# The first of eight groups in a product of a transformer block: from seven products of sums to eight plain block products

## The chip, the cores and the metric

The kernel runs on one NeuronCore of a Trainium2 chip. The metric is the device time of one execution in microseconds. TensorE (PE) multiplies, VectorE (DVE), ScalarE (ACT) and GpSimd (POOL) compute elementwise, SyncE (SP) issues DMAs; ACT and POOL issue some too. Each engine works through its own queue in order, and waits on the others through semaphores.

## The reference, cut to what matters

One decoder layer over 512 positions of width 1024, in float32: two attention branches, gates and an output projection, and then the MLP, in whose second product the change lies.

```python
h2 = rmsnorm(x, mlp_norm_g[l])                                   # (512, 1024)
x = x + jnp.square(jax.nn.relu(h2 @ w_ff1[l])) @ w_ff2[l]        # w_ff1 (1024, 4096), w_ff2 (4096, 1024)
...
return rmsnorm(x, final_norm_g)
```

## The kernel before, in words

Every product is made of float32 operands that are split in a high part (rounded to the matmul's format) and a low part (the rest): `mm3` runs three matmuls for each pair of operands, high x high, high x low and low x high. The high part is a copy on ACT, the low part a subtraction on DVE.

The hidden width 4096 is cut in 32 chunks of 128 rows; `ff1(f)` makes one: its weights are loaded (SP) and split (L119 on ACT, L121 on DVE, into three buffers each), PE runs 8 x 3 = 24 matmuls into an accumulator `pt` (two banks; the first three chunks, made early, use `pl`), and ACT applies Relu and Square (L913, L914) into a tile z. Four chunks make a group, so there are NG = 8 groups; a group has two tiles, z0 and z1 of 256 rows each.

The second product adds, for each group, z (512 positions x 512 rows) times a 512 x 1024 block of `w_ff2` to `acc`, which starts as x. It is a 2 x 2 block product, with A11 to A22 out of z0 and z1, and B11 to B22 (each 256 x 512, loaded by `raw`) out of `w_ff2`. Groups 0 to 6 do it in seven products instead of eight, on sums of blocks. The sums S1 to S4 of the z blocks are made on DVE (`asum`, L939). The sums T1 to T4 of the weight blocks are made by DMA (`tsum`): SP loads one block (L928), and a DMA of POOL's queue adds another onto it (L929). T1 is B11 + B12 and T3 is B12 + B22, T2 adds T3 onto B11, and T4 adds T2 onto B21, so T2 and T4 are sums of sums. `put_a` splits an A operand (L953, L954), `put_b` a B operand (L961, L962, five buffers). `pair(g, k)` runs product k of `ORDER`, 2 x 6 matmuls. Its results go on DVE to `acc`, or to two more accumulators, U and V, that are shared by all groups and come into `acc` by `last_sums` at the end; group 0 begins U and V with a copy (L989). One addition within `acc` (L1163, on POOL) prepares its lower half for that. The last group, 7, is done plainly: `last_put` splits z0 and z1 whole, and `last_group` runs eight block products of 4 x 3 matmuls.

PE's order is the order of the code. There `group(g)` puts the pairs of group g between the ff1 chunks of group g + 1. The other engines' and queues' order is set by a scheduler of the framework when the kernel is built, from the same code; waits come from the buffers and data. Pools that matter: `raw` and `t` tiles three each, `b` tiles five, `pl` four banks, `pt` two.

Of the kernel before, what the change touches and what calls it, by code (L numbers as in the profile page):

```python
# [10 lines left out]
F32 = mybir.dt.float32  # L11
F32R = mybir.dt.float32r
BF16 = mybir.dt.bfloat16
I32 = mybir.dt.int32
AF = mybir.ActivationFunctionType
ALU = mybir.AluOpType
# [4 lines left out]
S, D, DFF = 512, 1024, 4096  # L21
NB = S // 128
# [27 lines left out]
def body(nc, tc, ctx, a, out, dbg=lambda name, ap: None):  # L50
# [20 lines left out]
    def utile(i, dt, name):  # L71
        return u_p.tile([128, 4, S], dt, tag=f"u{i}", name=name)
# [11 lines left out]
    def pl_tile():  # L84
        return psL.tile([128, S], F32, tag="pl", name="pl")
# [52 lines left out]
    def mm3(ps, parts):  # L138
        n = len(parts)
        for i, (lh, ll, rh, rl) in enumerate(parts):  # L140
            pe.matmul(ps, lh, rh, start=(i == 0), stop=False)  # L141
            pe.matmul(ps, lh, rl, start=False, stop=False)  # L142
            pe.matmul(ps, ll, rh, start=False, stop=(i == n - 1))  # L143
# [27 lines left out]
    k = 0  # L171
# [99 lines left out]
    for c in range(2):  # L271
        dve.tensor_tensor(ang[:, c], bc(post[:, :, None], [128, NB, 16]), bc(invf[:, None, :], [128, NB, 16]),
                          op=ALU.mult)
# [617 lines left out]
    NG = 8  # L891
# [29 lines left out]
    def raw(g, key):  # L921
        r = RAW[g, key] = wt_p.tile([128, 2, 512], F32, tag="raw", name=key, bufs=3)
        sp.dma_start(r, wsrc(g, key))
# [31 lines left out]
        AS[g, "op", k] = (hi, lo)  # L955

    def put_b(g, k):
        key = ORDER[k][1] if g < NG - 1 else LASTB[k]
        x = (RAW if key[0] == "B" else TT)[g, key]
        t = bs_p.tile([128, 2, 2, 512], F32R, tag="b", name="b", bufs=NBS)  # L960
        act.activation(t[:, 0], x, AF.Copy)  # L961
        dve.tensor_tensor(t[:, 1], x, t[:, 0].bitcast(F32), op=ALU.subtract)  # L962
        BS[g, k] = (t[:, 0], t[:, 1])

    BLOCK = {0: (0, 0), 1: (0, 0), 4: (0, 1), 5: (1, 1), 6: (1, 0)}

    copied = {}

    def unit(g, k, m, cuts=(0, 512)):
        p = pl_tile()  # L970
        ah, al = AS[g, "op", k]
        bh, bl = BS[g, k]
        ms = slice(m * 128, (m + 1) * 128)
        for lo, hi in zip(cuts, cuts[1:]):
            c = slice(lo, hi)
            mm3(p[:, c], [(ah[:, q, ms], al[:, q, ms], bh[:, q, c], bl[:, q, c]) for q in range(2)])
            i, n = BLOCK.get(k, (0, 0))
            b = 2 * i + m
            cs = slice(512 * n + lo, 512 * n + hi)
            if k in BLOCK:  # L980
                t = acc[:, b, cs]
                if k == 5:
                    dve.tensor_tensor(t, t, p[:, c], op=ALU.subtract)
                else:
                    dve.tensor_tensor(t, p[:, c], t, op=ALU.add)
            t = {0: U, 2: V, 3: U}.get(k)
            if t is not None:
                if g == 0 and k != 3:
                    copied[k] = dve.tensor_copy(t[:, m], p)  # L989
                else:  # L990
                    dve.tensor_tensor(t[:, m], p[:, c], t[:, m], op=ALU.add)  # L991


    LASTB = ("B11", "B21", "B12", "B22")

    def last_put(j):
        t = utile(j, F32R, "al")
        hi, lo = t[:, 0:2], t[:, 2:4]
        act.activation(hi, Z[NG - 1, j], AF.Copy)
        dve.tensor_tensor(lo, Z[NG - 1, j], hi.bitcast(F32), op=ALU.subtract)  # L1000
        AS[j] = (hi, lo)

    def last_sums():
        for m in range(2):
# [6 lines left out]
            dve.tensor_tensor(c22, c22, uv, op=ALU.subtract)  # L1011

    def last_group():
        g = NG - 1
        for b in range(NB):
            ms = slice(b * 128, (b + 1) * 128)
            cuts = (0, 512, 768, 1024) if b == NB - 1 else (0, 512, 1024)
            for lo, hi in zip(cuts, cuts[1:]):
                n, cs = lo // 512, slice(lo, hi)
                c = slice(lo - 512 * n, hi - 512 * n)  # L1020
                p = pl_tile()[:, c]
                mm3(p, [(AS[j][0][:, q, ms], AS[j][1][:, q, ms], BS[g, 2 * n + j][0][:, q, c],
                         BS[g, 2 * n + j][1][:, q, c]) for j in range(2) for q in range(2)])
                dve.tensor_tensor(acc[:, b, cs], p, acc[:, b, cs], op=ALU.add)
                final(b, n, cs)

    def pair(g, k):
        for m in range(2):
            unit(g, k, m)

    def group(g):
        nxt = g + 1
        plain = nxt == NG - 1

        def nb():
            if bq:
                put_b(*bq.pop(0))

        def raws():
            for key in ("B11", "B21", "B12" if plain else "B22"):
                raw(nxt, key)

        if g == 0:
            put_a(g, 2)
            asum(g, "S4")
            ff1(4 * nxt)
            nb()
            tsum(0, "T4")  # L1050
            pair(g, 0)
            put_a(g, 3)
            pair(g, 1)
            with tc.issue_after(copied[0].ins):
                nb()
            put_a(g, 4)
            ff1(4 * nxt + 1)
            put_a(nxt, 0)
            nb()
            pair(g, 2)  # L1060
            raws()
            nb()
            nb()
            for key in ("T1", "T3", "T2"):
                tsum(nxt, key)
        else:
            pair(g, 0)
            raws()
            put_a(g, 2)
            asum(g, "S4")  # L1070
            ff1(4 * nxt)
            nb()
            pair(g, 1)
            nb()
            if not plain:
                for key in ("T1", "T3", "T2"):
                    tsum(nxt, key)
            put_a(g, 3)
            pair(g, 2)
            nb()  # L1080
            put_a(g, 4)
            ff1(4 * nxt + 1)
            if not plain:
                put_a(nxt, 0)
        put_a(g, 5)
        pair(g, 3)
        nb()
        put_a(g, 6)
        pair(g, 4)
        nb()  # L1090
        if plain:
            raw(nxt, "B22")
        else:
            tsum(nxt, "T4")
        ff1(4 * nxt + 2)
        if plain:
            last_put(0)
            ff1(4 * nxt + 3)
            last_put(1)
        pair(g, 5)  # L1100
        nb()
        if not plain:
            ff1(4 * nxt + 3)
            asum(nxt, "S1")
            asum(nxt, "S2")
        pair(g, 6)
        nb()
        if plain:
            last_sums()
        else:  # L1110
            asum(nxt, "S3")
            put_a(nxt, 1)
# [3 lines left out]
    def final(b, n, cs):  # L1116
        e = parts[b]
        parts[b] += 1
        o = fo[b]
        s3 = ss3[:, 3 * b:3 * b + 3]  # L1120
        act.activation(o[:, cs], acc[:, b, cs], AF.Square, accum_out=s3[:, e:e + 1])
        if e == 0:
            pool.tensor_tensor(xf[b], acc[:, b, cs], gf[:, cs], op=ALU.mult)
            dve.tensor_scalar(s3[:, 0:1], s3[:, 0:1], D * EPS, None, op0=ALU.add)
            first0[b] = cs.start
        if e == 0 or cs.stop % 512:
            if e:
                dve.tensor_tensor(s3[:, 0:1], s3[:, 0:1], s3[:, 1:2], op=ALU.add)
            return
        r = r3[:, b:b + 1]  # L1130
        pool.tensor_tensor(r, s3[:, e:e + 1], s3[:, 0:1], op=ALU.add)
        pool.tensor_tensor(r, r, mhalf[:, 0:1], op=ALU.pow)
        rows = slice(b * 128, (b + 1) * 128)
        step = 256 if b == NB - 1 else 512
        f0 = first0[b]
        for lo in range(0, 512, step):
            q = slice(f0 + lo, f0 + lo + step)
            act.activation(o[:, q], xf[b][:, lo:lo + step], AF.Copy, scale=r)
            act.dma_start(out[rows, q], o[:, q])
        for lo in range(512 - f0, 1024 - f0, step):  # L1140
            q = slice(lo, lo + step)
            dve.scalar_tensor_tensor(o[:, q], acc[:, b, q], r, gf[:, q], op0=ALU.mult, op1=ALU.mult)
            sp.dma_start(out[rows, q], o[:, q])
# [16 lines left out]
    first0 = {}  # L1160
    U = z_p.tile([128, 2, 512], F32, name="U")
    V = z_p.tile([128, 2, 512], F32, name="V")
    pool.tensor_tensor(acc[:, 2:4, :512], acc[:, 2:4, :512], acc[:, 2:4, 512:], op=ALU.add)  # L1163
    for key in ("B11", "B21", "B22"):
        raw(0, key)
    for key in ("T1", "T3", "T2"):
        tsum(0, key)
    bq = [(g, k) for g in range(NG) for k in range(NP if g < NG - 1 else 4)]
    for j in range(4):
        ff1(j, p0[j] if j < 3 else None)  # L1170
        if j == 1:
            put_a(0, 0)
    put_b(*bq.pop(0))
    put_b(*bq.pop(0))
    for i in range(3):
        asum(0, f"S{i + 1}")
    put_a(0, 1)
    for g in range(NG - 1):
        group(g)
    uo = [utile(4 + i, F32, f"o{i}") for i in range(4)]  # L1180
    fo = [uo[b // 2][:, 2 * (b % 2):2 * (b % 2) + 2].rearrange("p a b -> p (a b)") for b in range(NB)]
# [52 lines left out]
```

## Time and profile before

| | us |
|---|---|
| median of 3 runs | 712.93 (712.91 to 714.23) |
| the profiled execution | 712.22 |
| its span, first to last instruction | 710.5 |

A profile is one execution. In it, "idle before, releaser" is the time that an engine stood still ahead of an instruction and what ended that wait. Windows give each engine's busy time within a stretch and the clock that was granted to TensorE as a share of full speed. The ends of matmuls are modelled, so the pace of PE is read from where they start. Times are from the start of the span. The second MLP product begins at 388.79, after the first product has been running since the output projection ended.

### The profile page before, as it was taken

What the parts mean: (1) busy time and instruction counts of PE and PEld (TensorE: products, weight loads), DVE (VectorE), ACT (ScalarE), POOL (GpSimd) and SP (SyncE); (2) the same over time, 40 slices, a digit from 0 to 9 for tenths busy, and PEclk for the clock granted to TensorE, in tenths of its full rate; (3) what the DMA queues carried; (4) which work ended last, traced back from release to release, by engine and by line L of the source; (5) the groups of instructions that cost most, each with busy time, mean ns of one, the idle gap of its engine ahead of it and who ended that gap; (6) DMA issues with size and microseconds to landing.
All of it is one profiled execution on the core that took longest, in us unless ns stands there. A gap on an engine that the chain in (4) does not pass through costs nothing.

```text
span 710.5 us, 10170 instructions
## 1 busy us (share of the span) xinstructions
PE 688.9 (97%) x3665; PEld 558.0 (79%) x3666; DVE 512.4 (72%) x940; ACT 359.1 (51%) x619; POOL 191.9 (27%) x235
## 2 busy tenths in 40 slices
PE   8999999999999999999999499999999999999996
PEld 7879788768765777888898288888888888888885
DVE  6487899999999875783324586859586785859563
ACT  6466777654634455661224635444454555436333
POOL 2315387664156441320011011101001111000132
PEclk9999999999999999999999699999999999999999
DMA  8632522113211118881029687876869686761112
GB/s 320 226 112 90 153 92 75 46 45 103 83 68 45 47 61 308 293 277 55 1 95 272 167 234 211 225 191 172 228 160 238 149 229 185 171 156 30 31 47 102
DMA packets 41587, 102.88 MB, mean 145 GB/s; under 512 B 4352, under 2 KB 5248, under 8 KB 41536
## 3 DMA queue, kind: packets, MB, share of 16 engines
q1 hardware_dynamic: 34848, 86.47, 36.5%
q0 software_dynamic: 5824, 14.68, 12.2%
q10 hardware_dynamic: 864, 1.08, 0.4%
q8 instruction: 29, 0.48, 0.3%
q14 instruction: 22, 0.18, 0.1%
HBM read 87.66 MB, written 6.29 MB: 132 GB/s over the span
## 4 chain that ended last, share of the span: by engine, by line
PE 80%; DVE 13%; DMA 3%; issue 2%; ACT 1%; POOL 1%; SPq 0%; POOLq 0%; DVEq 0%; ACTq 0%
PE pl L143 11%; PE pl L141 11%; PE pl L142 11%; PE pt L141 7%; PE pt L142 7%; PE pt L143 7%; PE pl L237 3%; PE pl L239 3%; PE pl L238 3%; DVE nmx L590 2%; DVE oh L714 2%; PE pl L848 2%; PE pl L846 2%; PE pl L847 2%; DVE sc L401 2%; DVE m L400 2%
## 5 line engine op out<-in xcount | busy, mean ns | idle before, releaser
L119 ACT ACTIVATE whi<-wraw 128x1024 fp32r<-128x1024 f32 (+1 forms) x71 | 74.6, 1051 | 106.7 <-PE pt L142 90.2
L121 DVE TENSOR_TENSOR wlo<-wraw,whi 128x1024 fp32r<-128x1024 f32 (+1 forms) x60 | 73.8, 1232 | 72.1 <-ACT whi L119 72.0
L141 PE MATMUL pt<-h2h,whi 128*128 128x512 f32 x232 | 90.3, 389 | 0.0
L142 PE MATMUL pt<-h2l,whi 128*128 128x512 f32 x232 | 90.3, 389 | 0.0
L143 PE MATMUL pt<-h2h,wlo 128*128 128x512 f32 x232 | 90.2, 389 | 0.0
L141 PE MATMUL pl<-b,as 128*128 128x512 f32 x196 | 77.4, 395 | 8.7 <-ACT as L953 8.7
L143 PE MATMUL pl<-b,as 128*128 128x512 f32 x196 | 77.2, 394 | 1.6 <-DVE as L954 1.6
L142 PE MATMUL pl<-b,as 128*128 128x512 f32 x196 | 77.2, 394 | 0.0
L929 POOL DMA_DIRECT2D T<-wff x14 | 17.1, 1225 | 127.4 <-DVE V L991 50.3
L141 PEld LDWEIGHTS pt<-h2h,whi 128*128 128x128 f32 x232 | 43.6, 188 | 9.1
L143 PEld LDWEIGHTS pt<-h2h,wlo 128*128 128x128 f32 x232 | 43.6, 188 | 9.1
L142 PEld LDWEIGHTS pt<-h2l,whi 128*128 128x128 f32 x232 | 43.6, 188 | 8.9
L141 PEld LDWEIGHTS pl<-b,as 128*128 128x128 f32 x196 | 37.3, 190 | 16.8 <-ACT as L953 9.1
L961 ACT ACTIVATE b<-T 128x1024 fp32r<-128x1024 f32 x28 | 29.6, 1057 | 37.5 <-PE pl L143 16.0
L714 DVE TENSOR_SCALAR oh<-posbc,thr 128x400 bf16<-128x400 f32 (+31 forms) x128 | 45.7, 410 | 3.8 <-PE pl L735 3.7
L143 PEld LDWEIGHTS pl<-b,as 128*128 128x128 f32 x196 | 37.3, 190 | 10.1 <-DVE as L954 2.3
L237 PE MATMUL pl<-hh,whi 128*128 128x512 f32 x112 | 44.8, 400 | 0.0
L595 POOL TENSOR_SCALAR pra<-pra,rs 128x400 f32<-128x400 f32 (+31 forms) x32 | 35.2, 1110 | 35.0 <-DVE rs L594 35.0
L962 DVE TENSOR_TENSOR b<-T,b 128x1024 fp32r<-128x1024 f32 x28 | 34.1, 1222 | 13.7 <-ACT b L961 13.6
L239 PE MATMUL pl<-hh,wlo 128*128 128x512 f32 x112 | 43.7, 390 | 0.0
L238 PE MATMUL pl<-hl,whi 128*128 128x512 f32 x112 | 43.7, 390 | 0.0
L142 PEld LDWEIGHTS pl<-b,as 128*128 128x128 f32 x196 | 37.4, 191 | 7.7
(324 smaller groups left out, 1685.2 us busy)
## 6 DMA issues: line engine op xcount, KB each, us to landing
wraw<-wff SPq DMA_DIRECT2D x32, 512.0 KB, 4.2
T<-wff SPq DMA_DIRECT2D x28, 512.0 KB, 4.8
B<-wff SPq DMA_DIRECT2D x25, 512.0 KB, 5.8
wraw<-wF SPq DMA_DIRECT2D x24, 512.0 KB, 3.3
T<-wff POOLq DMA_DIRECT2D x14, 512.0 KB, 8.5
T<-T POOLq DMA_DIRECT2D x14, 512.0 KB, 5.7
gd<-gt SPq DMA_DIRECT2D x16, 256.0 KB, 2.2
wraw<-wbr SPq DMA_DIRECT2D x8, 512.0 KB, 4.0
```

What stands on the lines that cost most here:

```text
L119: act.activation(hi, raw, AF.Copy)
L121: eng.tensor_tensor(lo, raw, hi.bitcast(F32), op=ALU.subtract)
L141: pe.matmul(ps, lh, rh, start=(i == 0), stop=False)
L142: pe.matmul(ps, lh, rl, start=False, stop=False)
L143: pe.matmul(ps, ll, rh, start=False, stop=(i == n - 1))
L237: pe.matmul(p, h[:, k], hh[k], start=(k == 0), stop=False)
L238: pe.matmul(p, h[:, k], hl[k], start=False, stop=False)
L239: pe.matmul(p, l[:, k], hh[k], start=False, stop=(k == NK - 1))
L595: pool.tensor_scalar(pr, pr, rs, None, op0=ALU.mult)
L714: dve.tensor_scalar(oh[:, :n], posbc[:, :n], thr[:, 4 * G + q:4 * G + q + 1], None, op0=ALU.is_le)
L961: act.activation(t[:, 0], x, AF.Copy)
L962: dve.tensor_tensor(t[:, 1], x, t[:, 0].bitcast(F32), op=ALU.subtract)
```

## The change

Group 0 is done plainly, as the last group is: no S and T sums, four raw blocks in the order B11, B21, B12, B22, and eight block products of 12 matmuls, two at a time between the chunks ff1(4) to ff1(7). `plain_put` and `plain_block` are `last_put` and the body of `last_group` for any group. Group 1 is now the first to use U and V and begins them by the copy (L987 of the changed kernel). The addition within `acc` moves from ahead of group 0 to behind its blocks (L1069). The loads and sums for group 1 are written between the blocks of group 0.

```diff
-        key = ORDER[k][1] if g < NG - 1 else LASTB[k]
+        key = ORDER[k][1] if 0 < g < NG - 1 else PLAINB[k]
...
-                if g == 0 and k != 3:
-                    copied[k] = dve.tensor_copy(t[:, m], p)
+                if g == 1 and k != 3:
+                    dve.tensor_copy(t[:, m], p)
...
+    def plain_put(g, j):
+        t = utile(2 * (g == 0) + j, F32R, "al")
         hi, lo = t[:, 0:2], t[:, 2:4]
+        act.activation(hi, Z[g, j], AF.Copy)
+        dve.tensor_tensor(lo, Z[g, j], hi.bitcast(F32), op=ALU.subtract)
+        AS[g, "plain", j] = (hi, lo)
+
+    def plain_block(g, b, lo, hi):
+        ms = slice(b * 128, (b + 1) * 128)
+        n, cs = lo // 512, slice(lo, hi)
+        c = slice(lo - 512 * n, hi - 512 * n)
+        p = pl_tile()[:, c]
+        parts_ = []
+        for j in range(2):
+            ah, al = AS[g, "plain", j]
+            bh, bl = BS[g, 2 * n + j]
+            parts_ += [(ah[:, q, ms], al[:, q, ms], bh[:, q, c], bl[:, q, c]) for q in range(2)]
+        mm3(p, parts_)
+        dve.tensor_tensor(acc[:, b, cs], p, acc[:, b, cs], op=ALU.add)
...
+    def first_group():
+        blocks = [(b, 512 * n) for n in range(2) for b in range(NB)]
+
+        def two():
+            for _ in range(2):
+                b, lo = blocks.pop(0)
+                plain_block(0, b, lo, lo + 512)
+
+        ff1(4)
+        two()
+        for key in ("B11", "B21", "B22"):
+            raw(1, key)
+        for key in ("T1", "T3", "T2"):
+            tsum(1, key)
+        ff1(5)
+        put_a(1, 0)
+        two()
+        for _ in range(3):
+            nb()
+        tsum(1, "T4")
+        ff1(6)
+        two()
+        ff1(7)
+        asum(1, "S1")
+        asum(1, "S2")
+        two()
+        nb()
+        nb()
+        asum(1, "S3")
+        put_a(1, 1)
+        pool.tensor_tensor(acc[:, 2:4, :512], acc[:, 2:4, :512], acc[:, 2:4, 512:], op=ALU.add)
...
-    pool.tensor_tensor(acc[:, 2:4, :512], acc[:, 2:4, :512], acc[:, 2:4, 512:], op=ALU.add)
-    for key in ("B11", "B21", "B22"):
+    for key in PLAINB:
         raw(0, key)
-    for key in ("T1", "T3", "T2"):
-        tsum(0, key)
-    bq = [(g, k) for g in range(NG) for k in range(NP if g < NG - 1 else 4)]
+    bq = [(g, k) for g in range(NG) for k in range(NP if 0 < g < NG - 1 else 4)]
     for j in range(4):
         ff1(j, p0[j] if j < 3 else None)
-        if j == 1:
-            put_a(0, 0)
-    put_b(*bq.pop(0))
-    put_b(*bq.pop(0))
-    for i in range(3):
-        asum(0, f"S{i + 1}")
-    put_a(0, 1)
-    for g in range(NG - 1):
+        if j % 2:
+            plain_put(0, j // 2)
+            nb()
+            nb()
+    first_group()
+    for g in range(1, NG - 1):
         group(g)
```

How the order changes is seen on ACT from the middle of ff1's early chunks on. A row is a line, an operation, and output<-inputs; numbers tell buffers of one name apart. `b` is a split B operand, `as` an A operand, `al` a z tile split whole, `whi` the high part of a chunk's weights, `pt` ff1's accumulator. Before:

```order
L961 ACTIVATE b_4727<-T1_4609 128x1024
L914 ACTIVATE z1_4626<-z1_4626 128x512
L961 ACTIVATE b_4769<-T2_4615 128x1024
L913 ACTIVATE z1_4626<-pt_4647 128x512
L119 ACTIVATE whi_4695<-wraw_4693 128x1024
L914 ACTIVATE z1_4626<-z1_4626 128x512
L961 ACTIVATE b_4811<-B22_4607 128x1024
L953 ACTIVATE as_4623<-z1_4626 128x512
```

And of the change, from the conversion of B22 to the one of z1:

```order
L961 ACTIVATE b_4678<-B22_4608 128x1024
L1001 ACTIVATE al_4615<-z0_4610 128x1024
L913 ACTIVATE z1_4624<-pl_4476 128x512
L119 ACTIVATE whi_4641<-wraw_4639 128x1024
L914 ACTIVATE z1_4624<-z1_4624 128x512
L961 ACTIVATE b_4822<-B11_4743 128x1024
L119 ACTIVATE whi_4683<-wraw_4681 128x1024
L913 ACTIVATE z1_4624<-pt_4645 128x512
L914 ACTIVATE z1_4624<-z1_4624 128x512
L1001 ACTIVATE al_4672<-z1_4624 128x1024
```

The conversions of T1 and T2 stood ahead of z1's second half (made of `pt_4647`, which is ff1(3)); now a fourth raw block of group 0 and the first of group 1 stand there.

On SP's queue, from the first loads of the second product on, before:

```order
L923 DMA B22_4834<-wff2 128x2x512
L928 DMA T1_4842<-wff2 128x2x512
L112 DMA wraw_5128<-wff1 128x1024
L928 DMA T3_4845<-wff2 128x2x512
L928 DMA T2_4848<-wff2 128x2x512
```

These are group 1's (the row of B22 and those after it). Of the change, the rows around group 1's B22:

```order
L923 DMA B22_4747<-wff2 128x2x512
L112 DMA wraw_4758<-wff1 128x1024
L112 DMA wraw_4834<-wff1 128x1024
L112 DMA wraw_4896<-wff1 128x1024
L923 DMA B11_4990<-wff2 128x2x512
```

Group 1's T1, T3 and T2 now stand ahead of its B22, among the loads of group 0, and the weights of three ff1 chunks behind it.

## Rows read from the trace of the kernel before

**Rows 1.** Page, busy us (share of the span) and instructions of each engine.

```profile
PE 688.9 (97%) x3665; PEld 558.0 (79%) x3666; DVE 512.4 (72%) x940; ACT 359.1 (51%) x619; POOL 191.9 (27%) x235
```

**Rows 2.** Waits of PE: us in total, times, longest; the two longest.

```profile
PE pl L141 <- ACT as L953: 8.7, 1, 8.7
PE pl L143 <- DVE as L954: 1.6, 1, 1.6
```

**Rows 3.** Windows: stretch and length, busy us and instructions, granted clock, DMA.

```profile
core 0: us, PE busy (x) PEld busy (x) DVE busy (x) ACT busy (x) POOL busy (x), PEclk, DMA share, GB/s
...
388.79:437.41 48.62, 38.34 (x157) 30.74 (x156) 30.90 (x39) 22.96 (x31) 5.90 (x6) 0.86 0.77 208
...
400.36:407.48 7.12, 5.52 (x12) 3.89 (x13) 7.12 (x12) 5.46 (x9) 0.00 (x0) 0.51 0.50 151
...
440.00:680.00 240.00, 240.00 (x1061) 198.79 (x1060) 171.75 (x223) 114.09 (x150) 24.38 (x22) 1.00 0.65 167
```

**Rows 4.** Timeline of PE: start, us, line, operation, and idle before it.

```profile
391.29 0.39 PE L143 MATMUL pl<-b,as 128*128 128x512 f32 x1
400.36 0.79 PE L141 MATMUL pl<-b,as 128*128 128x512 f32 x1 [8.68 <-ACT as L953]
...
403.18 0.79 PE L143 MATMUL pl<-b,as 128*128 128x512 f32 x1 [1.60 <-DVE as L954]
403.77 0.63 PE L141 MATMUL pl<-b,as 128*128 128x512 f32 x1
...
407.18 0.46 PE L143 MATMUL pl<-b,as 128*128 128x512 f32 x1
407.48 0.40 PE L141 MATMUL pt<-h2h,whi 128*128 128x512 f32 x1
...
437.41 0.39 PE L141 MATMUL pl<-b,as 128*128 128x512 f32 x1
```

**Rows 5.** Chain of waits from 386 to 410: start, us, what.

```profile
378.14 12.02 DMA T<-wff
...
390.45 5.36 DMA T<-T
...
395.84 0.03 ACT b L961
```

**Rows 6.** Timeline of ACT, 371 to 397.

```profile
372.46 1.06 ACT L961 ACTIVATE b<-B 128x1024 fp32r<-128x1024 f32 x1 [0.33 <-DMA B<-wff]
...
386.10 1.06 ACT L961 ACTIVATE b<-T 128x1024 fp32r<-128x1024 f32 x1 [6.43 <-DMA T<-wff]
387.07 0.61 ACT L914 ACTIVATE z<-z 128x512 f32<-128x512 f32 x1
395.84 1.06 ACT L961 ACTIVATE b<-T 128x1024 fp32r<-128x1024 f32 x1 [8.16 <-DMA T<-T]
396.80 0.58 ACT L913 ACTIVATE z<-pt 128x512 f32<-128x512 f32 x1
```

**Rows 7.** Timeline of DVE: the low part of group 0's B11.

```profile
372.17 1.22 DVE L962 TENSOR_TENSOR b<-B,b 128x1024 fp32r<-128x1024 f32 x1 [4.12 <-ACT b L961]
```

**Rows 8.** SP's DMAs by time of issue (367, 377, 377.7): count, size, us to landing.

```profile
B<-wff SPq DMA_DIRECT2D x2, 512.0 KB, 5.3
...
B<-wff SPq DMA_DIRECT2D x2, 512.0 KB, 6.4
...
wraw<-wff SPq DMA_DIRECT2D x1, 512.0 KB, 12.1
```

**Rows 9.** Tile al of the last group: ns min/median/max, first and last start, forms.

```profile
L999 ACT ACTIVATE al<-z x2: 1061/1062/1062, 661.9 to 679.2; 128x1024 fp32r<-128x1024 f32 x2
L1000 DVE TENSOR_TENSOR al<-z,al x2: 1216/1218/1220, 664.0 to 680.3; 128x1024 fp32r<-128x1024 f32 x2
```

**Rows 10.** Timelines of POOL and of DVE: the POOL sum, a DVE subtraction beside POOL.

```profile
363.72 2.78 POOL L1163 TENSOR_TENSOR acc<-acc 128x1024 f32<-128x1024 f32 x1 [0.92 <-DVE xg L867]
...
683.77 1.18 DVE L1011 TENSOR_TENSOR acc<-acc,V 128x512 f32<-128x512 f32 x1
```

More of the change, by code (lines that the diff above doesn't have):

```diff
@@ L965, in body @@
     BLOCK = {0: (0, 0), 1: (0, 0), 4: (0, 1), 5: (1, 1), 6: (1, 0)}
-    copied = {}
     def unit(g, k, m, cuts=(0, 512)):
@@ L987, in unit, with pair @@
             if t is not None:
-                if g == 0 and k != 3:
-                    copied[k] = dve.tensor_copy(t[:, m], p)
+                if g == 1 and k != 3:
+                    dve.tensor_copy(t[:, m], p)
                 else:
                     dve.tensor_tensor(t[:, m], p[:, c], t[:, m], op=ALU.add)
-    LASTB = ("B11", "B21", "B12", "B22")
-    def last_put(j):
-        t = utile(j, F32R, "al")
-        hi, lo = t[:, 0:2], t[:, 2:4]
-        act.activation(hi, Z[NG - 1, j], AF.Copy)
-        dve.tensor_tensor(lo, Z[NG - 1, j], hi.bitcast(F32), op=ALU.subtract)
-        AS[j] = (hi, lo)
+    def pair(g, k):
+        for m in range(2):
+            unit(g, k, m)
+    PLAINB = ("B11", "B21", "B12", "B22")
+    def plain_put(g, j):
+        t = utile(2 * (g == 0) + j, F32R, "al")
+        hi, lo = t[:, 0:2], t[:, 2:4]
+        act.activation(hi, Z[g, j], AF.Copy)
[13 more added lines that the diff above has]
+        dve.tensor_tensor(acc[:, b, cs], p, acc[:, b, cs], op=ALU.add)
     def last_sums():
@@ L1013, in last_group, with nb @@
     def last_group():
-        g = NG - 1
         for b in range(NB):
-            ms = slice(b * 128, (b + 1) * 128)
             cuts = (0, 512, 768, 1024) if b == NB - 1 else (0, 512, 1024)
             for lo, hi in zip(cuts, cuts[1:]):
[L1019 to L1029, printed above, removed]
+                plain_block(NG - 1, b, lo, hi)
+                final(b, lo // 512, slice(lo, hi))
+    def nb():
+        if bq:
+            put_b(*bq.pop(0))
+    def first_group():
[27 more added lines that the diff above has]
+        pool.tensor_tensor(acc[:, 2:4, :512], acc[:, 2:4, :512], acc[:, 2:4, 512:], op=ALU.add)
     def group(g):
@@ L1035, in group @@
         plain = nxt == NG - 1
-        def nb():
-            if bq:
-                put_b(*bq.pop(0))
[L1041 to L1063, printed above, removed]
+        pair(g, 0)
+        for key in ("B11", "B21", "B12" if plain else "B22"):
+            raw(nxt, key)
+        put_a(g, 2)
+        asum(g, "S4")
+        ff1(4 * nxt)
+        nb()
+        pair(g, 1)
+        nb()
+        if not plain:
             for key in ("T1", "T3", "T2"):
                 tsum(nxt, key)
[L1066 to L1075, printed above, removed]
-                for key in ("T1", "T3", "T2"):
[L1077 to L1084, printed above, removed]
+        put_a(g, 3)
+        pair(g, 2)
+        nb()
+        put_a(g, 4)
+        ff1(4 * nxt + 1)
+        if not plain:
+            put_a(nxt, 0)
         put_a(g, 5)
@@ L1096, in group @@
         if plain:
-            last_put(0)
+            plain_put(nxt, 0)
             ff1(4 * nxt + 3)
-            last_put(1)
+            plain_put(nxt, 1)
         pair(g, 5)
@@ L1162, in body @@
     V = z_p.tile([128, 2, 512], F32, name="V")
-    pool.tensor_tensor(acc[:, 2:4, :512], acc[:, 2:4, :512], acc[:, 2:4, 512:], op=ALU.add)
-    for key in ("B11", "B21", "B22"):
+    for key in PLAINB:
         raw(0, key)
-    for key in ("T1", "T3", "T2"):
-        tsum(0, key)
-    bq = [(g, k) for g in range(NG) for k in range(NP if g < NG - 1 else 4)]
+    bq = [(g, k) for g in range(NG) for k in range(NP if 0 < g < NG - 1 else 4)]
     for j in range(4):
         ff1(j, p0[j] if j < 3 else None)
-        if j == 1:
-            put_a(0, 0)
-    put_b(*bq.pop(0))
-    put_b(*bq.pop(0))
-    for i in range(3):
-        asum(0, f"S{i + 1}")
-    put_a(0, 1)
-    for g in range(NG - 1):
+        if j % 2:
+            plain_put(0, j // 2)
+            nb()
+            nb()
+    first_group()
+    for g in range(1, NG - 1):
         group(g)
```

## The prediction

> **What bounds the kernel now.** Read the busy times first: PE is busy for 688.9 of 710.5 us [rows 1]. So the question is only where PE stands still, and the list of PE's waits answers it: two waits, 8.7 us on ACT and 1.6 us on DVE, are nearly all of them [rows 2]. The windows say where they are and what they cost. From 440 to 680 us PE is busy for 240.00 of 240.00 us at granted clock 1.00: groups 1 to 6 run without a hole. The stretch from 388.79 to 437.41, which is group 0 from its first product on, has 38.34 busy us in 48.62 and a mean clock of 0.86 [rows 3].
>
> The timeline of PE shows the shape of that hole: twelve matmuls of pair(0,0), the last at 391.29, then nothing until 400.36, another gap until 403.18, then matmuls that start 0.426 us apart ((407.18 - 403.77) / 8), and from 407.48 on the full pace [rows 4]. The full pace follows from the 132 matmuls between 407.48 and 437.41 (72 of three ff1 chunks, 60 of the pairs 2 to 6): 29.93 / 132 = 0.2267 us. The slow ones ran while the granted clock was 0.51, which is the lower of the two levels, 1.2 and 2.4 GHz [rows 3]; before it fell PE had stood still.
>
> The chain of waits names the cause. It comes from the DMA that sums T3 (378.14, 12.02 us), then the one that sums T2 out of T3 (390.45, 5.36 us), then ACT's conversion of T2 [rows 5]. In ACT's queue T2's conversion stands ahead of the activation of ff1(3), and so ahead of everything made from z1. ACT waits 6.43 us for T1 and 8.16 us for T2 and gets to z1 only at 396.80 [rows 6]. Pair(0,1) needs A12, which is made of z1; it doesn't need T2 at all.
>
> **The change part by part.**
>
> *Products.* Group 0 had 7 products x 2 row blocks x 6 matmuls = 84; eight plain blocks x 4 parts x 3 = 96. Twelve more, of the same shape. All lie on the path, since PE has no hole to put them in: 12 x 0.2267 = +2.72 us.
>
> *The stall.* From 388.79 to 437.41 PE runs 156 matmuls (84 of the pairs 0 to 6, 72 of ff1(5) to ff1(7)). At full pace they take 156 x 0.2267 = 35.37 us; the stretch takes 48.62. So 13.25 us are the two gaps and the slow matmuls after them. In the changed order ACT converts B11, B21, B12, B22 and the z tiles up to PE's first block, and nothing that is a DMA sum; the first sum (T1 of group 1) comes after ff1(5). If nothing takes the wait's place, all 13.25 us go.
>
> *Sum.* New stretch: 96 + 72 = 168 matmuls x 0.2267 = 38.08 us in place of 48.62, a gain of 10.54 us. Ahead of 388.79 PE runs the same instructions in both, and it ran them without a wait. The profiled execution took 712.22 us (span 710.5, so 1.72 around it): 712.22 - 10.54 = 701.7. The median of the runs, 712.93, is 0.7 above it; against that, 702.4. I take 702.4.
>
> *What is late next.* The first plain block starts on PE at 388.79. It needs z0's and z1's high and low parts and B11, B21. The low part of z1 is first read by its ninth matmul, at 388.79 + 8 x 0.2267 = 390.6. What could hold it up is B22: its tile is the fourth of a pool of three, so SP issues its load only after DVE made B11's low part, at 372.17 + 1.22 = 373.4 [rows 7], and ACT's conversion of B22 stands ahead of both z conversions. From B22's conversion to z1's high part ACT has six wide instructions (B22, z0, a ff1 weight, group 1's B11, another weight, z1) of at most 1.06 us and two pairs of Relu 0.58 and Square 0.61 [rows 6, 9]: 6.36 + 2.38 = 8.7 us, then 1.22 us on DVE for the low part [rows 9]. So B22 may land as late as 390.6 - 9.9 = 380.7. The price of the landing isn't shown before, since no fourth load stood there; the nearest rows are 5.3 us (the loads of 367 us), 6.4 us (the load behind one of weights, beside a DMA sum) and 12.1 us (a load behind three others, beside two sums) [rows 8]. I take 5.3 to 6.4, since ahead of B22 there is only what is left of T1's first load: landing at 378.7 to 379.8, 0.9 to 2.0 us early. The upper end, 373.4 + 12.1 = 385.5, would be 4.8 us late. The lower end is no gain, for PE has nothing to gain below full pace. Group 1's B11 waits in SP's queue behind B22 and stands in the same chain of ACT, five instructions (4.4 us) later: issued one low part (1.22 us) after B22, it may land at 385.1, and with 6.4 us it lands at 381.0.
>
> The Trainium skill (page "DMA: Bandwidth & Descriptors", section "Anatomy of one DMA — SWDGE (gpsimd) path") fits a transfer as 2.0 us plus its bytes over 436 GB/s, which for 512 KB makes an estimate of 3.2 us; by it B22 would land at 376.6, and rival 1 below would have no chance at all. The fit is for DMAs of the other path, and the rows of this trace are longer, 5.3 to 12.1 us for 512 KB; the rows decide.
>
> *Moved loads.* SP now issues group 1's B11, B21, B22 and T1 to T3 in the same stretch as group 0's blocks. Behind the last of them, which waits for B22's low part (about 381), stand the weights of ff1(7). Even at 12.1 us they land at 393, and ff1(7) begins after 120 more matmuls, at 388.79 + 27.2 = 416.0. Nothing lost; 20 us of cover. Group 0's four DMA sums and seven of its eleven loads fall away; PE is the bound after them, so I count nothing for it.
>
> *ACT beside PE.* Two conversions of weights now wait for the ff1 chunk that frees their buffer (for ff1(8) until ff1(5) ends, at 399.7), and behind them stand ff1's activations. These free the accumulators of ff1(6) and feed group 1, which are due at 405 and 426.9. Nothing lost.
>
> *The sum of acc's halves on POOL.* It took 2.78 us at 363.72 with little beside it; now it comes when the last plain block is added (about 427.5), beside DVE's busiest stretch. Next to such a POOL sum a DVE subtraction took 1.18 us [rows 10] in place of 0.69. DVE must empty the accumulators of pair(1,0) by 437.8, when pair(1,2) takes their banks; by DVE's order they are empty by about 433. Cover 4.7 us; if it were gone, at most 2.78 us.
>
> **The rivals.**
>
> *1. B22 lands late, and ACT holds up z1.* For it: ACT has just been seen waiting 6.43 and 8.16 us in order [rows 6], and T1's sum runs beside. Against it: B22's place in the queue. The point from which it decides is 380.7. At 12.1 us PE stands 4.8 us, and if the clock falls as before, 12 matmuls take 0.426 in place of 0.2267, 2.4 us more: 702.4 + 7.2 = 709.6. The middle, 706.
>
> *2. Slower: the stall goes along to group 1.* T2 of group 1 is still a sum of a sum, and ACT's conversion of it stands ahead of S4 and others. If it comes as late to ACT as T2 did before, the 13.25 us stay and the 12 matmuls come on top: 712.93 + 2.72 = 715.7. Place: pair(1,3). The point: T2 must be summed before pair(1,3), 84 matmuls (19.0 us) after group 1's start at 426.9, so by 445.9. Its first load is issued after B12's low part, near 378; with 12.1 us for that load, 12.0 for T3's sum and 5.4 for its own (in a row), it is there by 408. Against it stand nearly 38 us.
>
> *3. The change doesn't remove what it means to.* If PE's hole came from something other than the sums (say the weights' conversions, which stay), about as much would be lost as won: 712 to 714. The chain [rows 5] speaks against it.
>
> **How the numbers follow.** Forecast 702.4, chance 0.72. Rival 1, 703 to 709.6, 0.16. Rival 2, 715.7, 0.08. Rival 3, 0.04. Faster by over 0.2% (about what a measurement here tells from no change): 0.72 + 0.16 = 0.88; within 0.04; slower 0.08. The range begins at 701.2, half a microsecond below the sum against the profiled execution, and goes up to 707.5, which takes in some two thirds of rival 1.
>
> **What would show it.** In the changed profile, PE's waits above 1 us should be gone but for the first matmul of the kernel; from PE's first plain block to the first product of group 1 there should be 38.1 us at clock 1.00; group 1 should begin near 426.9. ACT's longest wait between 366 and 427 should be for PE, not for a DMA. Wrong would be: a PE gap at the first plain block behind ACT's z1 (rival 1, and B22's landing over 7.3 us), or one at pair(1,3) behind T2 (rival 2), or a group 1 that begins on time but is followed by waits of DVE's making at pair(1,2) (the POOL sum).

## The result, and the profile after

The changed kernel takes **702.04 us** (median of 4 runs, 701.69 to 702.46) against 713.58 us of the kernel before on the same chip (712.91 to 715.06, 4 runs): a ratio of 0.9836, 95% interval 0.9817 to 0.9854. The forecast was 702.4, in a range of 701.2 to 707.5. A second series, beside other runs of the kernel before, gave 702.38 (702.10 to 702.76, 5 runs).

The profiled execution took 701.69 us with a span of 700.0. The first fence is the page: busy us of each engine with its share of the span and instructions, then TensorE's granted clock over the span in 40 slices.

```profile
PE 689.0 (98%) x3677; PEld 559.2 (80%) x3678; DVE 502.8 (72%) x920; ACT 354.9 (51%) x611; POOL 185.4 (26%) x231
...
PEclk9999999999999999999999999999999999999999
```

PE is busy for as long as before (688.9 us in [rows 1]), with twelve more matmuls. It is the span that got shorter. That is no contradiction: the twelve added matmuls took the place of matmuls that ran at half pace. The list of PE's waits (total, times, longest) starts with these two:

```profile
PE pa L160 <- DVE warmb L157: 1.1, 1, 1.1
PE pt L625 <- ACT ptb L627: 0.7, 1, 0.7
```

The first is the kernel's first matmul, the second lies in the attention. The 8.7 and 1.6 us of [rows 2] have gone, and nothing stands in their place. The window from PE's first plain block to the first product of group 1 (columns as in [rows 3]) and the ends of that stretch in PE's timeline:

```profile
388.39:426.47 38.08, 38.08 (x169) 31.53 (x168) 14.88 (x19) 13.97 (x19) 1.75 (x2) 1.00 0.61 182
```

```profile
388.39 0.39 PE L141 MATMUL pl<-b,al 128*128 128x512 f32 x1
...
426.25 0.39 PE L143 MATMUL pl<-b,al 128*128 128x512 f32 x1
426.47 0.39 PE L141 MATMUL pl<-b,as 128*128 128x512 f32 x1
```

The answer to the 48.62 us at clock 0.86 of [rows 3] is 38.08 us, all of them busy, at clock 1.00. That is 168 matmuls at 0.2267 us, the sum of the prediction to the second decimal.

ACT's timeline shows the order that does it (start, us, instruction, and in brackets the wait ahead of it):

```profile
377.37 1.06 ACT L961 ACTIVATE b<-B 128x1024 fp32r<-128x1024 f32 x1
...
385.17 1.06 ACT L1001 ACTIVATE al<-z 128x1024 fp32r<-128x1024 f32 x1
391.67 1.06 ACT L119 ACTIVATE whi<-wraw 128x1024 fp32r<-128x1024 f32 x1 [5.45 <-DMA wraw<-wff]
...
421.00 1.06 ACT L119 ACTIVATE whi<-wraw 128x1024 fp32r<-128x1024 f32 x1 [8.67 <-PE pt L142]
...
425.78 1.04 ACT L961 ACTIVATE b<-T 128x1024 fp32r<-128x1024 f32 x1
```

B22 is converted at 377.37 and z1 at 385.17, where [rows 6] had ACT standing until 395.84 for T2. T2 of group 1, the sum of a sum, is converted at 425.78 with no bracket behind it: it had been there for long.

### The profile page after: what moved, and what is told of

Same layout as the page of the kernel before. It is cut to its first block, busy times and chain, and to the rows that moved or that the text cites. A ratio compares the mean times of both kernels' runs of the same rounds, so it can differ in the third digit from the quotient of the medians.

```text
span 700.0 us, 10136 instructions
## 1 busy us (share of the span) xinstructions
PE 689.0 (98%) x3677; PEld 559.2 (80%) x3678; DVE 502.8 (72%) x920; ACT 354.9 (51%) x611; POOL 185.4 (26%) x231
## 3 DMA queue, kind: packets, MB, share of 16 engines
q10 hardware_dynamic: 864, 1.08, 0.4%
## 4 chain that ended last, share of the span: by engine, by line
PE 83%; DVE 12%; issue 1%; POOL 1%; DMA 1%; ACT 1%; SPq 0%; POOLq 0%; DVEq 0%; ACTq 0%
PE pl L141 11%; PE pl L142 11%; PE pl L143 11%; PE pt L142 8%; PE pt L143 8%; PE pt L141 8%; PE pl L237 3%; PE pl L238 3%; PE pl L239 3%; DVE nmx L590 2%; DVE oh L714 2%; PE pl L847 2%; PE pl L846 2%; PE pl L848 2%; DVE sc L401 2%; DVE m L400 2%
## 5 line engine op out<-in xcount | busy, mean ns | idle before, releaser
L141 PE MATMUL pl<-b,as 128*128 128x512 f32 x168 | 65.4, 389 | 0.0
L142 PE MATMUL pl<-b,as 128*128 128x512 f32 x168 | 65.4, 389 | 0.0
L143 PE MATMUL pl<-b,as 128*128 128x512 f32 x168 | 65.4, 389 | 0.0
L929 POOL DMA_DIRECT2D T<-wff x12 | 14.7, 1229 | 102.8 <-DMA T<-wff 52.7
L929 POOL DMA_DIRECT2D T<-T x12 | 10.6, 879 | 114.1 <-DVE U L989 33.3
L595 POOL TENSOR_SCALAR pr<-pr,rs 128x512 f32<-128x512 f32 (+3 forms) x32 | 35.4, 1120 | 14.0 <-DVE rs L594 14.0
L962 DVE TENSOR_TENSOR b<-B,b 128x1024 fp32r<-128x1024 f32 x26 | 34.5, 1329 | 5.7 <-ACT b L961 5.7
L141 PEld LDWEIGHTS pl<-b,as 128*128 128x128 f32 x168 | 31.5, 188 | 6.6
L142 PEld LDWEIGHTS pl<-b,as 128*128 128x128 f32 x168 | 31.5, 188 | 6.6
```

Of the source, the lines that this page charges most:

```text
L595: pool.tensor_scalar(pr, pr, rs, None, op0=ALU.mult)
L929: pool.dma_start(t, TT[g, y] if y[0] == "T" else wsrc(g, y), accum_op=ALU.add)
```

## Experiments

The kernels are built out of the kernel before or the changed one. Of each, the edit is shown, then what was on record before it ran.

### The sums taken away, with T2's place on ACT kept

The theory was that ACT, which works in order, stood for T1 and T2 in front of z1. In the kernel before, group 0's T tiles lose their second load, so that they land as plain loads (the second block is left out of the result). T2's conversion keeps its place ahead of z1; the scheduler moved those of T1 and B22 further ahead.

```diff
-        pool.dma_start(t, TT[g, y] if y[0] == "T" else wsrc(g, y), accum_op=ALU.add)
+        if g:
+            pool.dma_start(t, TT[g, y] if y[0] == "T" else wsrc(g, y), accum_op=ALU.add)
```

> The kernel before, with group 0's four T tiles left as their first block (the DMA that adds the second block is left out for group 0), so that they land as plain loads, by about 377. T2's conversion still stands ahead of z1's second half on ACT. Theory (the sums' lateness, not the mere place, makes the wait): no stall, 699.3. Rival (place alone, or the weights' conversions beside it): 712 to 714.

It took 698.69 us (698.21 to 699.13), ratio 0.9788 [0.9761, 0.9815]. ACT's timeline:

```profile
380.13 1.05 ACT L962 ACTIVATE b<-T 128x1024 fp32r<-128x1024 f32 x1
...
384.07 0.58 ACT L913 ACTIVATE z<-pt 128x512 f32<-128x512 f32 x1
```

T2's conversion still stands ahead of z1, and costs nothing, since its data is there: ACT doesn't wait for it, and PE has no wait from 380 to 440. So the hole of the kernel before came from the sums that were late, and the whole price of it was about 14 us. This is also the floor for group 0 in seven products.

### The order changed, with the sums kept

If ACT's order is the other half of the cause, moving T1's and T2's conversions behind the A operands should be enough. This edit of the kernel before keeps the seven products; `issue_after` makes an engine take what is inside behind the instruction that is named.

```diff
...
-            put_a(g, 2)
+            s1 = put_a(g, 2)
...
-            nb()
+            with tc.issue_after(s1):
+                nb()
...
-            put_a(g, 3)
+            s2 = put_a(g, 3)
...
-            with tc.issue_after(copied[0].ins):
+            with tc.issue_after(s2):
                 nb()
```

> The kernel before, all seven products of group 0 kept. Only ACT's order is changed: T1's conversion is held behind that of S1, T2's behind that of S2, so that neither stands ahead of z1. Theory (ACT's wait for the DMA sums held up z1, 13.25 us; the twelve matmuls cost 2.72): the stall goes without them, 702.0 - 2.7 = 699.3, and PE has no wait near pair(0,1). Rival (the stall belongs to the first group's products of sums, whatever ACT's order): 712 to 714, with PE waiting for T2 or for an S at a later pair. Second rival (T2 is too late for its own product as well): PE waits at pair(0,3), 700 to 706.

It took 703.41 us (703.02 to 705.55), ratio 0.9861 [0.983, 0.9891]: 9.3 us of the hoped for 13.3. The old waits are gone, but PE's list now begins with this one, at the first matmul of pair(0,4):

```profile
PE pl L141 <- DVE V L990: 3.0, 1, 3.0
```

The timeline of POOL's queue, then of ACT, then of DVE show how it came about:

```profile
377.98 1.21 POOL L929 DMA_DIRECT2D T<-wff  x1 [0.40 <-issue]
393.21 0.90 POOL L929 DMA_DIRECT2D T<-T  x1 [14.02 <-DMA T<-wff]
```

```profile
398.55 1.06 ACT L962 ACTIVATE b<-T 128x1024 fp32r<-128x1024 f32 x1 [9.09 <-DMA T<-T]
```

```profile
399.64 1.23 DVE L963 TENSOR_TENSOR b<-T,b 128x1024 fp32r<-128x1024 f32 x1 [5.18 <-ACT b L962]
...
402.72 1.22 DVE L121 TENSOR_TENSOR wlo<-wraw,whi 128x1024 fp32r<-128x1024 f32 x1
403.86 1.22 DVE L963 TENSOR_TENSOR b<-B,b 128x1024 fp32r<-128x1024 f32 x1
405.00 2.35 DVE L963 TENSOR_TENSOR b<-T,b 128x1024 fp32r<-128x1024 f32 x2
...
407.87 0.68 DVE L990 COPY V<-pl 128x512 f32<-128x512 f32 x1
```

T3's sum, issued at 377.98, released the next one only at 393.21, and T2 was there at 398.55. ACT stood 9.09 us for it and DVE 5.18 us behind ACT. The work that piled up behind them, the first copy into V among it, came late, and that copy frees the PSUM bank that PE wanted at 405.5. The theory held for the two waits it named; what it overlooked is that T2 still stood ahead of other work. The time lies in the range of the second rival, but PE didn't wait at pair(0,3) for T2, as that rival had it.

Two further versions tried to clear the queues. The next one holds the DVE halves of T3 and T4 behind the copies into V as well.

```diff
             pair(g, 2)
             raws()
-            nb()
-            nb()
+            with tc.issue_after(copied[2].ins):
+                nb()
+                nb()
```

> The kernel before with the two moves of e1_order (the conversions of group 0's T1 and T2 held behind the two operand conversions that PE's next products read), and one more: the DVE halves of the two last B conversions of group 0 (T3 and T4) are held behind the two copies into V, which empty the PSUM banks that PE waited 3.0 us for in e1_order. Theory (e1_order fell short only because those copies stood in DVE's queue behind the B conversions, which themselves stood behind the late sum): the wait at PE of 3.0 us at 410 goes, and the time is 703.4 - 3.0 = 700.4 us or a little less, down to 699.3, the time before less its 13.25 us of waits and of slow matmuls. Rival (the late sum itself is what limits, and the wait only moves to the next product, the one that reads the T2 or the T3 operand): the time stays at 702.5 to 704.0 us, with a wait of PE of 2 us or more on a b operand.

It was worse: 707.49 us (706.07 to 708.47), ratio 0.9918 [0.9898, 0.9937]. The rival's time is passed too, so neither account was right. DVE's queue shows why: what moved up ahead of the copy was the low half of a weight, whose high half ACT made only at 405.39.

```profile
406.47 1.23 DVE L121 TENSOR_TENSOR wlo<-wraw,whi 128x1024 fp32r<-128x1024 f32 x1
407.61 0.68 DVE L990 COPY V<-pl 128x512 f32<-128x512 f32 x1
```

PE waited 2.95 us for the bank again, and this time slow matmuls followed (see the last section). It also waited 1.60 us at 439.76, in pair(1,1), for a z1 operand of group 1: ACT had stood 12.14 us, until 432.65, for group 1's T2.

> The changed kernel as it is, on the same chip as e8_order2 for a direct comparison: 702.0 us, as its four runs gave (701.7 to 702.5). If the theory of e8_order2 holds, e8_order2 is ahead of it by 1.5 to 2.7 us: it saves the same stall and does not pay for the 12 added matmuls of 0.2267 us (2.72 us). By the rival e8_order2 is no faster than this.

The changed kernel on the same chip: 702.38 us (702.10 to 702.76), ratio 0.9849 [0.9827, 0.987], as expected; the order of the two came out by the rival.

The last version moves the cause itself. T1's conversion stays behind S1's operand. T2's goes behind S4's operand and the activations of the next group, the others of B22, T3 and T4 behind A11's operand on ACT and behind the copies on DVE.

```diff
-            with tc.issue_after(copied[0].ins):
-                nb()
-            put_a(g, 4)
+            s4 = put_a(g, 4)
             ff1(4 * nxt + 1)
-            put_a(nxt, 0)
-            nb()
+            with tc.issue_after(s4):
+                nb()
+            s5 = put_a(nxt, 0)
             pair(g, 2)
             raws()
-            nb()
-            nb()
+            with tc.issue_after(copied[2].ins), tc.issue_after(s5):
+                nb()
+                nb()
+                nb()
```

> The kernel before, with ACT's conversion of group 0's T1 held behind the operand conversion of S1, that of T2 held later than in e1_order, behind the operand conversion of S4 (so that the first stage's activation of the next group and a weight conversion don't stand behind the late sum), and those of B22, T3 and T4 behind the operand conversion of the next group's A11, with their DVE halves behind the two copies into V. Theory (in e1_order and e8_order2 everything that PE waited for stood in ACT's or DVE's queue behind the conversion of the late T2; with the queues cleared ahead of it nothing is late any more): no wait of PE at 380 to 440, 699.3 us, the time before less its 13.25 us of waits and slow matmuls, up to 700.3. Rival (T2's sum lands too late for its own product, whatever the queues, or the last conversions of the group come late in turn): a wait of PE on a b operand of 1 us or more, with slow matmuls behind it, and 701.5 to 705 us.

The profiled execution took 700.75 us (span 699.0). In group 0 PE loses no more than 0.3 us; the copy into V comes at 402.31 instead of 407.87. DVE's timeline:

```profile
398.82 1.23 DVE L963 TENSOR_TENSOR b<-T,b 128x1024 fp32r<-128x1024 f32 x1 [2.56 <-ACT b L962]
...
402.31 0.68 DVE L990 COPY V<-pl 128x512 f32<-128x512 f32 x1
```

But the hole opened anew in group 1, smaller. The timelines of ACT and of PE:

```profile
427.02 1.06 ACT L962 ACTIVATE b<-T 128x1024 fp32r<-128x1024 f32 x1 [7.89 <-DMA T<-T]
...
428.93 0.58 ACT L913 ACTIVATE z<-pt 128x512 f32<-128x512 f32 x1
```

```profile
434.13 0.50 PE L143 MATMUL pl<-b,as 128*128 128x512 f32 x1 [1.02 <-DVE as L954]
```

Group 1's T2 stands ahead of group 1's z1 on ACT, just as group 0's did in the kernel before, and PE waits in pair(1,1) for the low part that is made of z1. Neither account on record names this wait. Against a start every 0.2267 us PE loses 1.8 us between 380 and 460, 1.2 of them here; without them the span would be 697.2, and the run without sums had 697.0. The sum of group 1's T2 was issued at 420.74 here, and at 391.89 in the changed kernel. So the change does a second thing: it has group 1's sums issued earlier. What that alone is worth was not tried.

The five runs lie between 700.75 and 704.16, with a median of 702.41, ratio 0.9855 [0.9828, 0.9881]: the median is that of the changed kernel, and no version with group 0's sums was shown to beat it. The profiled execution is the fastest of the five; what made the other four longer was not seen, since only one execution has a trace. The versions with sums in group 0 all scatter (before: 710.9 to 715.4 over these series), while the changed kernel stays within 701.7 to 702.8 over nine runs and the version without sums within 698.2 to 699.1. That would fit sums that land later in some runs, which ACT still waits for, but it is an inference.

### The wait put back into the changed kernel

If ACT's standing in front of z1 is the mechanism, one small instruction should restore it. In the changed kernel ACT reads one column of group 1's T2 ahead of z1's conversion; its loads and sums are written ahead of that.

```diff
...
+        if j == 3:
+            for key in ("B11", "B21", "B22"):
+                raw(1, key)
+            for key in ("T1", "T3", "T2"):
+                tsum(1, key)
+            wait = act.activation(warm, TT[1, "T2"][:, 0, 0:1], AF.Copy)
+            with tc.issue_after(wait.ins):
+                plain_put(0, 1)
```

> The changed kernel, with one ACT instruction of one column added, which reads group 1's summed T2 and stands ahead of z1's conversion; nothing else is computed from it. Theory: ACT waits for T2's sum, which landed near 400.4 in the changed kernel, z1's low part comes near 403 instead of 387.5, and PE stands some 13 us behind its sixth plain matmul, plus up to 2.4 us at the lower clock: 714 to 718. Rival (the plain products are what helped, by whatever else they changed): 702 to 704.

It took 715.31 us (714.44 to 715.77, 10 runs), ratio 1.003 [1.0012, 1.0047]. ACT's timeline, and PE's:

```profile
399.55 0.20 ACT L1183 ACTIVATE warm<-T 128x1 f32<-128x1 f32 x1 [13.59 <-DMA T<-T]
```

```profile
400.75 0.80 PE L141 MATMUL pl<-b,al 128*128 128x512 f32 x1 [10.01 <-ACT al L1001]
...
402.60 0.63 PE L141 MATMUL pl<-b,al 128*128 128x512 f32 x1
403.03 0.63 PE L142 MATMUL pl<-b,al 128*128 128x512 f32 x1
```

An instruction of 0.20 us gives back the hole, the slow matmuls 0.43 us apart, and more than all of the gain. The 715.3 us are the 702.0 of the changed kernel and 13.3 us, as much as the stretch of the kernel before held. They are also close to the 715.7 that the prediction gave to its rival 2, whose late T2 is put in ACT's way by hand here, though at group 0's first block and not at pair(1,3).

### The cover of z1, and what happens when it is used up

The prediction named z1's lateness as what would decide. Copies of z1 onto itself on ACT, in the changed kernel, push it back, first two and then four.

```diff
     def plain_put(g, j):
...
+        if (g, j) == (0, 1):
+            for _ in range(2):
+                act.activation(Z[g, j], Z[g, j], AF.Copy)
```

> The changed kernel, with two copies of z1 onto itself on ACT (1.06 us and some 0.05 between) ahead of its conversion. In the changed kernel z1's low part was made by 387.49 and first read at 390.20, so there are 2.7 us of cover. Theory: 2.2 us later, all within the cover, 702.0. Rival (no cover: PE waits on z1 already, unseen): 704.2.

> The same with four copies; a Relu of the next group (0.5 us) comes between as well. Theory: z1's low part by 392.4, 2.2 us after it is first read: PE waits 2.2 us in two pieces, 704.2, with the clock kept at 1.00 for so short a wait. Rival 1 (the clock falls as it did after the long wait): up to 2.4 us more, 706.6. Rival 2 (no cover): 706.9.

With two copies it took 702.18 us (702.05 to 702.54), ratio 0.9842 [0.9826, 0.9858]: no loss, so the cover exceeds two copies. With four it took 704.88 (704.00 to 705.72), ratio 0.9879 [0.986, 0.9898]. PE's timeline with four:

```profile
391.46 0.50 PE L141 MATMUL pl<-b,al 128*128 128x512 f32 x1 [1.07 <-ACT al L1004]
...
392.72 0.69 PE L143 MATMUL pl<-b,al 128*128 128x512 f32 x1 [0.53 <-DVE al L1005]
393.21 0.63 PE L141 MATMUL pl<-b,al 128*128 128x512 f32 x1
...
396.19 0.44 PE L142 MATMUL pl<-b,al 128*128 128x512 f32 x1
396.47 0.40 PE L143 MATMUL pl<-b,al 128*128 128x512 f32 x1
```

The waits are 1.6 us, but from 393.21 to 396.19 the matmuls start 2.98 / 7 = 0.426 us apart. At the matmul of 396.70, the nineteenth from 388.87, PE is 396.70 - (388.87 + 18 x 0.2267) = 3.75 us behind, over twice the waits. The runs' median lies between the two times that were on record, with the profiled run, the longest of the four, near the upper one. The granted clock over the whole run was 0.995 in the two longer runs (705.72 and 705.30) and 0.998 in the two shorter (704.45 and 704.00). That fits slow matmuls in two of the four runs only, though one alone has a trace.

### The price of twelve matmuls, and of POOL's addition

In the changed kernel, one plain block's twelve matmuls run twice. In a second edit POOL's addition within `acc` goes back to its old place ahead of the blocks.

```diff
     def plain_block(g, b, lo, hi):
...
+        if (g, b, n) == (0, 3, 1):
+            mm3(p, parts_)
         mm3(p, parts_)
```

> The changed kernel, with the last plain block's twelve matmuls run twice into the same accumulator (the second run starts it anew). Theory (each matmul of this stretch lies on the path at 0.2267 us): 702.0 + 2.7 = 704.8. Rival (PE has slack there, and something else sets the start of group 1): under 703.

```diff
     def first_group():
...
-        pool.tensor_tensor(acc[:, 2:4, :512], acc[:, 2:4, :512], acc[:, 2:4, 512:], op=ALU.add)
...
     V = z_p.tile([128, 2, 512], F32, name="V")
+    pool.tensor_tensor(acc[:, 2:4, :512], acc[:, 2:4, :512], acc[:, 2:4, 512:], op=ALU.add)
```

> The changed kernel, with POOL's addition within acc moved back ahead of the blocks, where it stood before (so the blocks' part of it is left out of the result). Theory (DVE's delay beside it is covered): the DVE instruction that took 3.42 us beside it takes 1.22 again, and the time stays, 702.0. Rival (it holds up group 1): 699.8 to 701.

Twelve more matmuls made 704.79 us (704.50 to 705.07), 2.75 more than the 702.04 of the changed kernel, where 12 x 0.2267 = 2.72. The addition moved back made 701.86 (701.69 to 701.93), which is no difference that can be told. It is seen on DVE, in the subtraction behind which the accumulators of pair(1,0) are emptied. The rows of the changed kernel are POOL's addition, then DVE's subtraction; the last fence is that subtraction in the edited kernel.

```profile
427.69 3.31 POOL L1069 TENSOR_TENSOR acc<-acc 128x1024 f32<-128x1024 f32 x1 [14.34 <-DVE acc L1016]
```

```profile
428.66 3.42 DVE L962 TENSOR_TENSOR b<-B,b 128x1024 fp32r<-128x1024 f32 x1
...
433.80 0.67 DVE L987 COPY U<-pl 128x512 f32<-128x512 f32 x1
```

```profile
428.83 1.21 DVE L962 TENSOR_TENSOR b<-B,b 128x1024 fp32r<-128x1024 f32 x1
```

The subtraction takes 3.42 us beside the addition and ends about when it does; without it, it takes 1.21.

## Why the prediction was right, point by point

**The products.** 2.72 us for the twelve matmuls; the doubled block measured 2.75.

**The stall.** 13.25 us was read from one stretch of one trace. Two experiments stand on either side of it: with the wait put back, 715.31 - 702.04 = 13.3; with the sums taken away, 712.74 (the median of before in that series) - 698.69 = 14.05. The second is larger by 0.8, within the scatter of the runs of before.

**The sum.** The stretch took 38.08 us, as worked out. It began 0.40 us earlier than in the kernel before (388.39 against 388.79), which the prediction had not counted, and from its end to the end of the span 0.44 us were lost. The last matmuls show where: 6.94 us lie between the last matmul's start and the end (700.0 - 693.06) in the changed kernel, 6.50 (710.5 - 704.00) in the one before. The timeline of PE in the changed kernel and then in the one before:

```profile
693.06 0.28 PE L143 MATMUL pl<-b,al 128*128 128x256 f32 x1
```

```profile
704.00 0.28 PE L143 MATMUL pl<-b,al 128*128 128x256 f32 x1
```

The two cancel. The span fell by 10.5 us and the gain of the sum is 10.54, so the sum was right in part because two small terms that it lacked were equal. By the medians the gain is larger, 713.58 - 702.04 = 11.54. The forecast carried over the 0.7 us by which the median of the kernel before lay above its profiled execution; the changed kernel's lies 0.35 above, so 702.4 came out 0.36 too high.

**B22, the term that was bounded.** The bounds were 5.3 and 12.1 us for its landing, and 5.3 to 6.4 was taken. SP's queue issued it in a pair of loads from 372.51 on:

```profile
372.51 1.77 SPq L923 DMA_DIRECT2D B<-wff  x2
```

ACT converted it at 377.37 without waiting, so it landed in at most 4.9 us, below the lower bound. The four other B loads that SP issued behind it, up to 395, took 5.7, 8.2, 10.1 and 11.9 us, each longer than the one before, which fits the argument from its place in the queue. The chain on ACT behind it was rightly sized: from 377.37 to z1's end at 386.23 are 8.86 us, with a wait of 0.65 for PE in it, where 8.7 were summed. DVE's low part of z1:

```profile
386.26 1.23 DVE L1002 TENSOR_TENSOR al<-z,al 128x1024 fp32r<-128x1024 f32 x1 [1.02 <-ACT al L1001]
```

It ended at 387.49 and PE's ninth matmul read it at 388.39 + 8 x 0.2267 = 390.2: a cover of 2.7 us, where 0.9 to 2.0 were expected. The two copies fit into it and the four did not, so the cover is real and not wide. Rival 1 was the right one to fear. Its price is confirmed in kind by the four copies: in the profiled run the clock's part came on top of waits of 1.6 us too, and more than doubled them.

**Rival 2** had its point at 445.9 and a bound of 408 for T2 of group 1. The sum was issued at 391.89 and took 8.5 us, so it landed at 400.4, where 5.4 had been put for it. These are POOL's timeline and the DMA view of the changed kernel (count, size, us to landing), of 372 to 395:

```profile
391.89 0.90 POOL L929 DMA_DIRECT2D T<-T  x1 [9.26 <-DMA T<-wff]
```

```profile
T<-wff POOLq DMA_DIRECT2D x2, 512.0 KB, 10.0
T<-T POOLq DMA_DIRECT2D x1, 512.0 KB, 8.5
```

The sum is no faster than that of group 0's T2 was before (5.36 us in [rows 5]). It has become harmless because it is issued early, at 391.89 against 427.08 for the same sum before, and nobody needs it for another 25 us. Where it was issued at 420.74, in the last of the reordered versions, a wait of this kind did come, though at pair(1,1) and not at pair(1,3): group 1's z1 stood behind T2 in ACT's queue, which the rival hadn't looked at.

**Rival 3** is excluded by the run without sums: 698.69 with all the weights' conversions in place.

**The signs that were named.** ACT's longest wait from 366 to 427 is the 8.67 us for PE, as forecast; beside it stands one of 5.45 us for a DMA, the weights that the prediction let land at 393 at the latest. They landed at 391.6. DVE waited 5.28 us behind their conversion, and PE not at all.

**POOL's addition** was under-priced. The prediction took 1.18 us for a DVE subtraction of 512 columns beside POOL, read from one row of [rows 10], where only the last 0.6 us of a POOL instruction of half that size lay beside it (682.26 and 2.14 us, to 684.40); one of 1024 columns was held for 3.42, and the addition itself took 3.31 in place of 2.78. The banks were empty at 434.5, due at 426.47 + 48 x 0.2267 = 437.35: a cover of 2.9 us in place of 4.7. It was enough.

## What to carry to other kernels

An engine that works in order passes the lateness of one operand on to everything behind it. So ask not only when a late result is read, but what stands behind the reader in its queue: here twelve more matmuls bought the time that a conversion of 1.06 us had cost, and one read of 0.20 us gave it all back. Moving the late reader is worth trying before paying with arithmetic, but each move puts another instruction ahead of a third one, or brings the next group's late operand into the way, and none of three versions here cleared all the waits. Price a stall of PE at more than its waits, since the matmuls behind it may run at half pace.

## What the hardware showed that was not expected

**The clock after short waits.** Waits of 1.07 and 0.53 us were followed by matmuls at half pace with four copies of z1. A wait of 2.95 us was followed by them in one version with its order changed, and one of 3.03 us was not in another. The windows of these three, in that order (columns as in [rows 3]; the last figures are the granted clock, the DMA share and GB/s):

```profile
393.21:396.47 3.26, 3.26 (x10) 2.57 (x8) 1.73 (x2) 0.00 (x0) 0.18 (x1) 0.53 1.07 384
```

```profile
408.44:412.39 3.95, 3.95 (x11) 3.09 (x11) 3.95 (x6) 1.69 (x2) 0.82 (x1) 0.57 1.04 306
```

```profile
408.70:412.00 3.30, 3.22 (x13) 2.35 (x14) 3.30 (x5) 1.40 (x2) 0.68 (x1) 1.00 0.99 334
```

In the last of the reordered versions 1.02 us left the granted clock at 1.00 as well (430 to 440). So the length of the wait alone didn't decide whether the clock fell to the lower of its levels (1.2 of 2.4 GHz) behind it. What did was not tried, and no price for a wait of 1 to 3 us follows but a range: its own length, or up to a little over twice that (3.75 us for waits of 1.6).

**DVE beside POOL.** A DVE subtraction with two inputs in SBUF took 3.42 us instead of 1.21 when POOL's addition had begun a microsecond earlier. POOL's addition ended at 431.00 and the subtraction at 432.08. The Trainium skill (page "SBUF — State Buffer", section "Who interferes with whom") says that the two share a pair of ports, that a DVE instruction with two SBUF inputs contends with a POOL instruction that reads SBUF, and that the order of issue decides which of them blocks; the trace agrees: the one that came second was delayed by 2.2 us and ended 1.08 us behind the other, about its own length.

**Sums by DMA.** A sum of 512 KB onto a tile took about 15 us from issue to release in one version (377.98 to 393.21) and 10.0 us (median of two) in the changed kernel. Plain loads of that size took from at most 4.9 us (B22) to 11.9 there, so it isn't shown that the adding itself makes a transfer longer. T2 needs T3's sum first, so two of them come in a row.
